# A row sum bound by its loads: one whole first load in front of the entry barrier, a wait for the ends moved forward, and a store of its own for the first seven blocks

## The chip, the cores and the metric

The kernel runs on one core of one Trainium2 chip. The time is device microseconds of that core. A profile adds its own clock: "span" is the time from the first to the last instruction on the core, about 1.8 us less than the device time. All runs quoted here are of the fast state, with a granted clock of 1.0.

Some words. A DMA moves data between memory and the core; SyncE issues it, and the core's 16 DMA engines carry it in packets. A semaphore is a counter on which an engine waits; the semaphore of a DMA tells that its data has landed. The entry barrier is the place at the program's start where all engines wait for each other. A nop is an instruction that does nothing, but can wait.

## The reference

```python
batch, seq, dim = 32, 512, 1024          # x: float32, standard normal
def reference(x, multiplier):            # multiplier = 0.5
    return (np.sum(x, axis=-1) * multiplier).astype(np.float32)
```

So 16,384 rows of 4 KB (67.1 MB) are read, and 64 KB of sums are written.

## The kernel before

Each of the 128 partitions owns 128 consecutive rows. A block is 16 rows of every partition, 8.4 MB; there are eight blocks and three buffers. In blocks 0 to 6 VectorE (DVE) sums the first eight rows with one reduction and ScalarE (ACT) the other eight with one ACTIVATE each. The last block comes in five pieces that get smaller and smaller. All DMAs are issued by SyncE (SP).

```python
    x_rows = x_flat.rearrange("(p c) d -> p c d", p=P)
    out_view = out.rearrange("b s -> (b s)").rearrange("(p c) -> p c", p=P)
    ...
    for b in range(n_blocks - 1):
        c0 = b * B
        t = x_pool.tile([P, B, D], fp32, name="xb")
        step = 4 if b == 0 else 1
        for q in range(step):                       # block 0: every fourth partition
            nc.sync.dma_start(
                out=t[q:P:step], in_=x_rows[q:P:step, c0 : c0 + B, :]
            )
        h = B // 2
        nc.vector.reduce_sum(out=sums[:, c0 : c0 + h], in_=t[:, 0:h, :], ...)
        nc.vector.tensor_single_scalar(out=res[:, c0 : c0 + h], ...)
        for r in range(h, B):
            act_row(t, r, c0 + r)
    ...
    pieces = [(0, 8), (8, 13), (13, 15)]            # the last block, rows;
    ...                                             # row 15 in columns 0:640, 640:1024
    nc.sync.dma_start(out=out_view, in_=res)        # 64 KB, after everything

    def start_loads_at_entry(nc_):
        ...          # moves SP's leading loads that wait for nothing in front of
        ...          # SP's part of the entry barrier
            for i in own:
                if not is_load(i) or i.sync_info.on_wait:
                    break
                lead.append(i)
```

Six loads can go without waiting: four pieces of block 0, block 1, block 2. All six are issued in front of the entry barrier.

## Time and profile before

| | before |
|---|---|
| device time | 163.19 us median of three (163.19 to 163.27) |
| span of the profiled run | 161.6 us (that run took 163.42 us) |
| DVE, ACT busy | 42% each |
| loads' share of the chain of waits | 85% |
| mean DMA rate | 416 GB/s |

The page says at once what the bound is. These are its lines for the busy share in 40 slices (tenths) and the DMA rate, of the kernel before:

```profile
DVE  0000039800596007940099101990039800597453
ACT  0000039900595007920099101990039700596852
...
DMA  6989989988989988998998997997997997999990
GB/s 260 519 373 406 519 373 405 519 389 389 519 357 422 519 389 389 519 405 373 519 422 359 519 438 341 519 438 341 519 438 341 519 438 341 430 438 398 424 375 28
```

DVE and ACT stand still more than half of the time (busy 42% each); the DMA engines, whose packets fill 96.7% of 16 engines' span, hardly ever do, except in the first slice and in the last. The trace's packet records give the pace: a 64 KB packet, one partition's share of a block, takes 2.418 us in the median on each of 16 engines. That is 27.1 GB/s per engine and, by multiplication, 434 GB/s together. With the engines that busy (a share of 0.98 from 10 to 40 us) nothing in the middle can be gained by waiting less. What is open is the head, before all 16 engines move data, and the tail, after the last data.

The tail, from the end of the chain that ended last (start, length, what) in the kernel before:

```profile
110.47 47.68 DMA xb<-in_x_dram
158.15 0.02 issue
158.18 0.49 DVE xb L57
...
158.76 0.42 DVE xb L57
159.18 0.01 DVEq L167
```

DVE is done at 159.18 us; the store and the closing barrier take the other 2.44 us to the span's end at 161.62. The store's own lines from the view of its source line, with durations in ns and starts in us:

```profile
L108 SPq EVENT_SEMAPHORE  x1: 17/17/17, 159.2 to 159.2; - x1
L108 SPq DMA_DIRECT2D out_dram<-res x1: 348/348/348, 159.3 to 159.3; - x1
```

The head: the DMA view cut to the first 4 us, in 40 slices of 0.1 us, and the first issue on SP's queue (start, length):

```profile
GB/s 0 0 0 0 0 0 0 0 0 0 0 0 0 1311 0 1966 1311 0 0 655 1311 1311 0 1311 0 655 655 0 0 0 0 0 0 0 0 0 0 0 0 0
...
0.00 0.54 SPq L73 DMA_DIRECT2D xb<-in_x_dram  x1
```

Each packet is counted in the slice in which it starts, so this row shows the starts: 655 is one packet of 64 KB. The first of the 16 engines starts at 1.36 us (slice 14), the last at 2.68 us. And the first reduction, which waits for all of block 0 (its last piece landed at 22.75 us, and DVE then went through waits for all four), starts at 22.87 us:

```profile
22.87 8.69 DVE L77 TENSOR_REDUCE sums<-xb 128x8 f32<-128x8192 f32 x1 [22.87 <-DMA xb<-in_x_dram]
```

### The profile page before, as it was taken

Reading aid. Unit: us, or ns where it says so; the run is one execution under the profiler, and the core shown is the slowest. Engines: PE = TensorE matmul, PEld = TensorE weight load, DVE = VectorE, ACT = ScalarE, POOL = GpSimd, SP = SyncE. Lnnn points to the kernel's source line nnn. Section 1 sums busy time; section 2 is a strip of 40 time slices with the busy share of each in tenths; the row PEclk is TensorE's granted clock in tenths of the full one; section 3 lists DMA queues with packets and bytes.
Section 4 is the critical chain, followed back from the end, with each engine's and each line's share of the span. In section 5 each row is a group of like instructions: output and inputs, shape, how many; then the busy total and the mean of one; then the engine's idle time right before and its main releaser. Section 6 shows DMA issues by size and latency. Waiting matters only on the chain.

```text
span 161.6 us, 242 instructions
## 1 busy us (share of the span) xinstructions
DVE 68.1 (42%) x34; ACT 67.9 (42%) x127; POOL 0.2 (0%) x4
## 2 busy tenths in 40 slices
DVE  0000039800596007940099101990039800597453
ACT  0000039900595007920099101990039700596852
POOL 0000000000000000000000000000000000000000
DMA  6989989988989988998998997997997997999990
GB/s 260 519 373 406 519 373 405 519 389 389 519 357 422 519 389 389 519 405 373 519 422 359 519 438 341 519 438 341 519 438 341 519 438 341 430 438 398 424 375 28
DMA packets 1921, 67.18 MB, mean 416 GB/s; under 512 B 256, under 2 KB 512, under 8 KB 640
## 3 DMA queue, kind: packets, MB, share of 16 engines
q1 hardware_dynamic: 1920, 67.18, 96.7%
q14 instruction: 1, 0.01, 0.0%
HBM read 67.11 MB, written 0.07 MB: 416 GB/s over the span
## 4 chain that ended last, share of the span: by engine, by line
DMA 85%; DVE 11%; SPq 2%; issue 0%; DVEq 0%
DMA xb<-in_x_dram 85%; DVE sums L77 11%; SPq L73 2%; SPq L94 1%; DVE xb L57 1%; DVE part L57 0%; DVEq L167 0%
## 5 line engine op out<-in xcount | busy, mean ns | idle before, releaser
L77 DVE TENSOR_REDUCE sums<-xb 128x8 f32<-128x8192 f32 x7 | 60.8, 8686 | 85.7 <-DMA xb<-in_x_dram 85.7
L47 ACT ACTIVATE xb<-xb 128x1024 f32<-128x1024 f32 x63 | 65.6, 1043 | 67.8 <-DMA xb<-in_x_dram 67.8
L47 ACT ACTIVATION_READ_ACCUMULATOR xb<-xb 128x1 f32 x63 | 11.8, 187 | 0.0
L47 ACT ACT_TABLE_LOAD x1 | 1.3, 1283 | 22.8 <-DMA xb<-in_x_dram 22.8
L57 DVE CUSTOM_DVE_ANT_0 xb<-xb 128x512 f32<-128x512 f32 (+1 forms) x9 | 5.6, 667 | 5.1 <-DMA xb<-in_x_dram 4.9
L80 DVE TENSOR_SCALAR res<-sums 128x8 f32<-128x8 f32 x7 | 1.2, 172 | 0.2
L57 DVE DVE_READ_ACCUMULATOR2_ANT res<- 128x1 f32 x9 | 0.7, 83 | 0.0
L57 DVE CUSTOM_DVE_ANT_0 xb<-xb,part 128x192 f32<-128x192 f32 x1 | 0.4, 418 | 0.1
L153 POOL MEMSET const-bfloat16-1.0<- 128x1 bf16 x1 | 0.1, 102 | 0.0
L153 POOL MEMSET const-uint8-127<- 128x1 uint8 x1 | 0.1, 102 | 0.0
L153 POOL MEMSET const-float32-0.0<- 128x1 f32 x1 | 0.1, 99 | 0.2 <-issue 0.2
L153 POOL MEMSET const-float32-1.0<- 128x1 f32 x1 | 0.1, 99 | 0.0
L57 DVE DVE_READ_ACCUMULATOR2_ANT part<- 128x1 f32 x1 | 0.1, 81 | 0.0
## 6 DMA issues: line engine op xcount, KB each, us to landing
xb<-in_x_dram SPq DMA_DIRECT2D x1, 4096.0 KB, 39.6
xb<-in_x_dram SPq DMA_DIRECT2D x1, 2560.0 KB, 45.4
xb<-in_x_dram SPq DMA_DIRECT2D x1, 1024.0 KB, 47.4
xb<-in_x_dram SPq DMA_DIRECT2D x1, 320.0 KB, 47.7
xb<-in_x_dram SPq DMA_DIRECT2D x1, 192.0 KB, 47.6
xb<-in_x_dram SPq DMA_DIRECT2D x10, 43.8
out_dram<-res SPq DMA_DIRECT2D x1, 64.0 KB, 1.5
```

Of the source, the lines that this page charges most:

```text
L47: nc.scalar.activation(out=t[:, r, :], in_=t[:, r, :], func=mybir.ActivationFunctionType.Copy, scale=mul, accum_out=res[:, col : col + 1],)
L57: nc.vector.tensor_tensor_reduce(out=t[:, r, lo:mid], in0=t[:, r, lo:mid], in1=t[:, r, mid:hi], scale=mul, scalar=start, op0=ADD, op1=ADD, ...
L73: nc.sync.dma_start(out=t[q:P:step], in_=x_rows[q:P:step, c0 : c0 + B, :])
L77: nc.vector.reduce_sum(out=sums[:, c0 : c0 + h], in_=t[:, 0:h, :], axis=mybir.AxisListType.X)
L80: nc.vector.tensor_single_scalar(out=res[:, c0 : c0 + h], in_=sums[:, c0 : c0 + h], scalar=mul, op=mybir.AluOpType.mult,)
L94: nc.sync.dma_start(out=t[:, lo:hi, :], in_=x_rows[:, c0 + lo : c0 + hi, :])
L153: nc = _bacc.Bacc("TRN2", target_bir_lowering=False, num_devices=1)
```

## The change

Its intent has three parts. Block 0 comes as one load, which alone stands in front of the entry barrier. The results of blocks 0 to 6 are stored by a DMA of their own while the last block is still coming, so that only 8 KB are left to store at the end. And a nop on SP waits for the loads and for ACT's last row before the last store, so that these waits are not left to the end of the program.

```diff
-        step = 4 if b == 0 else 1
-        for q in range(step):
-            nc.sync.dma_start(
-                out=t[q:P:step], in_=x_rows[q:P:step, c0 : c0 + B, :]
-            )
+        loads.append(nc.sync.dma_start(out=t, in_=x_rows[:, c0 : c0 + B, :]))
 ...
+    c1 = c0
+    nc.sync.dma_start(out=out_view[:, 0:c1], in_=res[:, 0:c1])
     on_act = {4, 5, 6, 7, 11, 12, 14}
 ...
-    nc.sync.dma_start(out=out_view, in_=res)
+    seen = nc.sync.nop()
+    for i in loads[-8:] + acts[-1:]:
+        tc.add_manual_dep(seen.ins, i.ins.name, ..., reason="ends seen early")
+    store = nc.sync.dma_start(out=out_view[:, c1:], in_=res[:, c1:])
+    tc.add_manual_dep(store.ins, seen.ins.name, ..., reason="in this order")
 ...
             for i in own:
-                if not is_load(i) or i.sync_info.on_wait:
+                if not is_load(i) or i.sync_info.on_wait or len(lead) == 1:
                     break
```

More of the change, by code (lines that the diff above doesn't have):

```diff
@@ L44 @@
     part = res_pool.tile([P, 1], fp32, name="part")
+    loads = []
+    acts = []
     def act_row(t, r, col):
-        nc.scalar.activation(
+        acts.append(nc.scalar.activation(
             out=t[:, r, :],
@@ L52, in act_row @@
             accum_out=res[:, col : col + 1],
-        )
+        ))
     def dve_span(t, r, lo, hi, dst, start=0.0):
@@ L70 @@
         t = x_pool.tile([P, B, D], fp32, name="xb")
-        step = 4 if b == 0 else 1
-        for q in range(step):
-            nc.sync.dma_start(
-                out=t[q:P:step], in_=x_rows[q:P:step, c0 : c0 + B, :]
-            )
+        loads.append(nc.sync.dma_start(out=t, in_=x_rows[:, c0 : c0 + B, :]))
         h = B // 2
@@ L93 @@
     for lo, hi in pieces:
-        nc.sync.dma_start(out=t[:, lo:hi, :], in_=x_rows[:, c0 + lo : c0 + hi, :])
+        loads.append(
+            nc.sync.dma_start(
+                out=t[:, lo:hi, :], in_=x_rows[:, c0 + lo : c0 + hi, :]
+            )
+        )
     for lo, hi in ((0, cut), (cut, D)):
-        nc.sync.dma_start(
-            out=t[:, B - 1, lo:hi], in_=x_rows[:, c0 + B - 1, lo:hi]
-        )
+        loads.append(
+            nc.sync.dma_start(
+                out=t[:, B - 1, lo:hi], in_=x_rows[:, c0 + B - 1, lo:hi]
+            )
+        )
+    c1 = c0
+    nc.sync.dma_start(out=out_view[:, 0:c1], in_=res[:, 0:c1])
     on_act = {4, 5, 6, 7, 11, 12, 14}
@@ L106, with start_load_at_entry @@
     dve_span(t, B - 1, cut, D, res[:, rows - 1 : rows], start=part)
-    nc.sync.dma_start(out=out_view, in_=res)
-    def start_loads_at_entry(nc_):
+    seen = nc.sync.nop()
+    for i in loads[-8:] + acts[-1:]:
+        tc.add_manual_dep(
+            seen.ins,
+            i.ins.name,
+            mybir.DependencyInfo(mybir.DependencyClass.Sync, mybir.DependencyReason.DATA),
+            reason="ends seen early",
+        )
+    store = nc.sync.dma_start(out=out_view[:, c1:], in_=res[:, c1:])
+    tc.add_manual_dep(
+        store.ins,
+        seen.ins.name,
+        mybir.DependencyInfo(mybir.DependencyClass.NoSync, mybir.DependencyReason.SCHED_ONLY),
+        reason="in this order",
+    )
+    def start_load_at_entry(nc_):
         entry, *rest = nc_.main_func.blocks
@@ L134, in start_loads_at_entry @@
             return
-    nc.at_finalize(start_loads_at_entry)
+    nc.at_finalize(start_load_at_entry)
 _INS = ['x', 'multiplier']
```

## The prediction

> **What bounds the kernel.** The load stream. The page's first two parts: DVE and ACT are busy 42% each, the DMA slices read 9 (96.7% of 16 engines' span), 67.18 MB at 416 GB/s. The chain of waits is 85% loads; DVE enters it only as the release of a buffer whose next load already queues behind others. The trace's packet records: a 64 KB packet takes 2.418 us (median), 27.1 GB/s on each of 16 engines. [...] An engine's 64 packets' worth need 154.8 us, so only about 6.9 us of the span are open: start and end.
>
> **Start.** The first packets of the 16 engines begin between 1.355 and 2.683 us; [...]last packets of the last load end between 157.05 and 158.18 us, the same 1.1 us spread. [...] Six load issues take 3.74 us there (0.54 to 0.76 each), and the starts fall while issues 3 to 5 are written. [...]the final store's packets begin 0.85 us after its issue, on all engines within about 0.2 us. I think a single first load, with nothing issued behind it until the barrier (about 1 us later by the barrier instructions' times), starts the engines closer together, perhaps by 1.2 to 2.2 us: estimated gain 0.4 us, anything from -0.5[...] to +1.0.
>
> **ACT's table load** (1.28 us at 22.84 us) waits in "before" for three of the four first loads; after, only the first ACTIVATE waits, so it hides at the start. Block 3's load may be issued 1 us earlier, but 40 us of loads queue before it: worth 0. Loads two and three, after the barrier, have 20 us of slack.
>
> **End.** Last landing 158.15, DVE's two pieces to 159.18 (unchanged), store issue 0.35, landing 1.5 us from issue (160.8), closing barrier 0.75. SP's waits for the other loads (six of 28 ns after the store's issue) already run inside the store's flight, so seeing them early gains at most about 0.05 us. The last store falls from 64 to 8 KB; its 27 ns packets x 8 per engine are 0.22 us of the flight, shrinking to perhaps 0.08: gain 0.1. The rest is fixed (this trace: 0.85 us before the first packet, about 0.35 us after the last). The early store is issued near 148 us behind the last loads in the same rings; its 8 packets per engine (estimate 0.2 us) come after the loads and before the last store: worth 0.
>
> **Sum.** 163.19 - 0.4 - 0.15 = 162.6 us, 8 in 10 within 161.8 to 163.5. Faster by over 2%: 0.03; within 2%: 0.94; slower by over 2%: 0.03.
>
> **What would show it.** Right: first packets of all engines within under 1 us; last landing at about 157.6 instead of 158.15; ACT_TABLE_LOAD before 3 us; the last store landing about 1.4 us from issue; DVE, ACT groups unchanged. Wrong: first packets still spread over 1.3 us (then only the end's 0.1 to 0.2 us comes), or the last landing later than 158.2.
>
> **What would make it wrong.** The cold start may be a cost of each engine's first read rather than of competing issues (no gain)[...]. The stores' 448- and 64-byte rows might write slowly.

Passages are cut where it is marked. What the runs show of the middle is that no kernel below has a median packet under 2.418 us. 163.19 - 0.4 - 0.15 = 162.64, put down as 162.6. The 0.4 us is the author's estimate: a last first packet at about 2.2 instead of 2.683 us would be 0.48 us earlier, and it was assumed, not shown, that the end moves with it. The 0.15 is the estimated 0.05 for the waits and 0.1 for the small store.

Three of its numbers are loose: the sixth issue took 0.46 us and not 0.54 or more, the first packets spread over 1.33 us and not 1.1, and the waits between the store's issue and the drain are five (one of 17 and four of 28 ns), of which four ran before the landing. "The same rings" are the one queue, q1, that the DMA view shows for all loads and stores.

## The result

| | before | after |
|---|---|---|
| device time, six fast runs each | 163.25 us (163.19 to 163.28) | 162.96 us (162.91 to 163.22) |
| ratio, 95% interval | | 0.9985 (0.9972 to 0.9998) |
| span of the profiled run | 161.6 us | 161.1 us |

All outputs are right. A ratio here is the mean time of one kernel's fast runs over the mean of the other's in the same rounds, so it is not quite the ratio of the medians quoted. In a later job the changed kernel ran again (e12): 162.90 us against 163.28, ratio 0.9979 (0.9967 to 0.9991). So the change gains about 0.3 us, 0.2%. The time lies in the predicted range; the predicted gain (0.55 us) was about twice the measured one. Note that the profiled run of before took 163.42 us, slower than its timed runs, and that of after 162.91, its fastest: the half microsecond between the two spans flatters the change.

The same views of the changed kernel. The end of its chain, its last store, its first 4 us and its first issue, its first reduction, and ACT's first instructions:

```profile
110.01 47.72 DMA xb<-in_x_dram
157.73 0.02 issue
157.75 0.49 DVE xb L60
...
158.32 0.42 DVE xb L60
158.74 0.01 DVEq L190
```

```profile
L125 SPq EVENT_SEMAPHORE  x2: 28/28/28, 158.8 to 158.8; - x2
L125 SPq DMA_DIRECT2D out_dram<-res x1: 344/344/344, 158.9 to 158.9; - x1
```

```profile
GB/s 0 0 0 0 0 0 0 0 0 0 2621 1966 655 655 0 655 1311 1311 1311 0 0 0 0 0 0 0 0 0 0 0 0 0 0 0 0 0 0 0 0 0
...
0.00 0.38 SPq L74 DMA_DIRECT2D xb<-in_x_dram  x1
...
22.55 8.69 DVE L76 TENSOR_REDUCE sums<-xb 128x8 f32<-128x8192 f32 x1 [22.55 <-DMA xb<-in_x_dram]
```

```profile
0.79 1.28 ACT L50 ACT_TABLE_LOAD   x1 [0.79 <-PEq L176]
22.55 1.06 ACT L50 ACTIVATE xb<-xb 128x1024 f32<-128x1024 f32 x1 [20.48 <-DMA xb<-in_x_dram]
```

The first packet starts at 1.02 us instead of 1.36, the first reduction at 22.55 us instead of 22.87 (block 0 landed at 22.53 instead of 22.75), the last load lands at 157.73 instead of 158.15, and DVE ends at 158.74 instead of 159.18. The tail from there to the span's end is 161.12 - 158.74 = 2.38 us instead of 2.44. ACT's table load (1.28 us) has moved from 22.84 to 0.79 us and is hidden. So the gain is in the load stream; 0.22 us of it is there when block 0 has landed, the rest comes later in these two profiles. The tail, at which two of the three parts of the change aim, gives 0.06 us. The experiments ask why the head starts earlier and why the tail gives so little.

### The profile page after: what moved, and what is told of

It is laid out like the page before. It is cut to its first block, busy times and chain, and to the rows that moved or that the text cites. A ratio compares the mean times of both kernels' runs of the same rounds, so it can differ in the third digit from the quotient of the medians.

```text
span 161.1 us, 236 instructions
## 1 busy us (share of the span) xinstructions
DVE 68.1 (42%) x34; ACT 67.9 (42%) x127; POOL 0.2 (0%) x4
## 4 chain that ended last, share of the span: by engine, by line
DMA 86%; DVE 11%; SPq 1%; issue 0%; DVEq 0%
DMA xb<-in_x_dram 86%; DVE sums L76 11%; SPq L94 1%; DVE xb L60 1%; SPq L74 0%; DVE part L60 0%; DVEq L190 0%
## 6 DMA issues: line engine op xcount, KB each, us to landing
out_dram<-res SPq DMA_DIRECT2D x1, 56.0 KB, 10.8
```

## The experiments

All diffs below are against the changed kernel. For the head there were two theories. P is that of the prediction: issues that follow each other compete, so the engines start late and far apart, and it helps to put one load alone in front of the barrier. T came from the two traces: in before the mean second packet of the engines took 2.53 us, in after the mean fifth 2.59 us, the others from the second on 2.42 or 2.43. T says that an engine's first read of a far region is slow and that cutting block 0 in four brings two such reads early. For the tail, A says that the head has most of the gain, its rival that the tail has it.

### The start alone (e1)

```diff
-    c1 = c0
-    nc.sync.dma_start(out=out_view[:, 0:c1], in_=res[:, 0:c1])
 ...                                      # the nop and its dependencies too
-    store = nc.sync.dma_start(out=out_view[:, c1:], in_=res[:, c1:])
+    nc.sync.dma_start(out=out_view, in_=res)
```

> The new start (one whole first load in front of the barrier) with the old end (one 64 KB store). Theory A, most of the gain is at the start: 0.15 to 0.25 us quicker than before, last landing about 157.75 us as in the changed kernel, tail from DVE's end to the span's end 2.44 us as before. Rival, the gain is the end's (smaller last store): within 0.05 us of before.

Measured: 163.30 us (163.09 to 163.64) against 163.33, ratio 0.9997 (0.9985 to 1.0010). By the time alone the rival would have won. But the profile shows the early landing: block 0 there at 22.30 us, last landing 157.63, DVE's end 158.68. This was the quickest of its five runs (163.09), so it shows the head at its best. The loss is behind that: from DVE's end to the span's end 2.63 us instead of before's 2.44, although the store is the same 64 KB and is issued equally soon (0.07 us) after DVE's end. These are SP's instructions between the store's landing and the closing drain; first before, then e1:

```profile
L167 SPq EVENT_SEMAPHORE  x1: 28/28/28, 160.8 to 160.8; - x1
L167 SPq DRAIN  x1: 7/7/7, 160.9 to 160.9; - x1
```

```profile
L174 SPq EVENT_SEMAPHORE  x4: 28/28/28, 160.3 to 160.5; - x4
L174 SPq DRAIN  x1: 7/7/7, 160.6 to 160.6; - x1
```

The last wait in before, and all four in e1, end after the landing; in e1 they are about 62 ns apart. The built programs of before and e1 say why. In them each DMA gets one of eight completion semaphores in turn, and the program's end waits for all of them in one order, the same in both, mostly two per instruction:

```
S3 | S4,S2 | S5,S1 | S6,S0 | S7,DVE | drain: ACT
```

In before 15 loads precede the store, so it has semaphore 7 and its wait is in the last pair. The whole first load leaves 12 loads; the store gets semaphore 4, its wait is in the second pair, and three more instructions run after the landing. Nothing in the source says so. The trace shows the inserted EVENT_SEMAPHORE instructions, at 28 ns each and about 62 ns from one to the next.

### The end alone (e2)

```diff
-        loads.append(nc.sync.dma_start(out=t, in_=x_rows[:, c0 : c0 + B, :]))
+        step = 4 if b == 0 else 1
+        for q in range(step):
+            loads.append(nc.sync.dma_start(
+                out=t[q:P:step], in_=x_rows[q:P:step, c0 : c0 + B, :]))
 ...
-                if not is_load(i) or i.sync_info.on_wait or len(lead) == 1:
+                if not is_load(i) or i.sync_info.on_wait:
```

> The old start (load cut in four, three blocks in front of the barrier) with the new end (early store, ends seen early). Theory A: 0.05 to 0.10 us quicker than before; with the start's gain it adds up to the changed kernel's 0.25. Rival: it has all of the gain.

Measured: 163.21 us (163.13 to 163.38) against 163.24, ratio 0.9996 (0.9984 to 1.0009): no resolved gain. The tail of its profile is 2.36 us, 0.08 less than before's, as theory A expected; a gain of that size can't be told from the noise. Theory A's other half, that the two parts add up to the whole, is not met by the times: each alone gives about nothing, both together 0.3 us. The waits of e1 explain 0.19 us of that; the intervals leave room for the rest.

### All three whole loads in front of the barrier (e3)

```diff
-                if not is_load(i) or i.sync_info.on_wait or len(lead) == 1:
+                if not is_load(i) or i.sync_info.on_wait:
```

> As the changed kernel, but all three first loads, each whole, in front of the barrier. If the place of the barrier matters (competing issues, or the barrier itself), the start falls back towards before: 0.2 us slower than the changed kernel. If only the way the first load is cut matters, the same as the changed kernel within 0.05 us. First packets at 1.0 to 1.9 us in both cases by my guess.

Measured: 162.94 us (162.85 to 163.16) against 163.33, ratio 0.9975 (0.9963 to 0.9988): as quick as the changed kernel. The second and third issue follow at 0.44 and 0.90 us, just before the engines' starts, and the starts don't mind (the first at 1.0 us, the last at 2.3):

```profile
GB/s 0 0 0 0 0 0 0 0 0 0 2621 1966 655 1311 0 655 1311 0 655 0 0 655 0 655 0 0 0 0 0 0 0 0 0 0 0 0 0 0 0 0
```

So "alone in front of the barrier" is worth nothing here, and theory P falls: two issues that follow the first whole load did not delay it (162.94 us here, 162.90 to 162.96 for the changed kernel).

### The cut in four behind the new barrier (e4)

```diff
+        step = 4 if b == 0 else 1        # as in e2
 ...
-                if not is_load(i) or i.sync_info.on_wait or len(lead) == 1:
+                if not is_load(i) or i.sync_info.on_wait or len(lead) == 4:
```

> As the changed kernel, but the first load is cut in four interleaved pieces as before, all four in front of the barrier, loads two and three behind it. Theory of competing issues (P): little gain, since four issues still follow each other: first packets spread 1.2 us or more. Theory of first touches (T: a DMA engine's first read of a far region is slow, and the cut in four makes packets one and two both first reads): the second packet's mean stays near 2.53 us and the time is about 0.2 us longer than the changed kernel's.

Measured: 163.38 us (163.04 to 163.73) against 163.33, ratio 1.0001 (0.9987 to 1.0014). With the cut, all of the gain is gone. The first packets start late, at 1.52 us, and the first reduction starts at 22.82 us:

```profile
GB/s 0 0 0 0 0 0 0 0 0 0 0 0 0 0 0 655 1966 0 655 1311 0 1311 1311 655 0 0 1311 655 0 655 0 0 0 0 0 0 0 0 0 0
```

The second packet's mean was 2.46 us, not 2.53, and in e2, with the same cut, 2.42. In the same way the fifth packet of the whole load was 2.42 us in e3, e6, e7 and e12. T's slow packets were thus a matter of single profiles, and T falls too. In after they are one burst: eight packets that started between 11.46 and 12.19 us took 2.69 to 2.94 us. Bursts of seven or eight packets that start within 0.7 to 0.8 us stand in other profiles at other moments: at 40.6 us in before (2.62 to 2.96 us), 25.8 in e12, 35.6 in e6, 31.1 in e4, none in e7 and e8. Their cause is open. What e3 and e4 leave is that the cut itself matters. I call that theory S: the shape of the first load (32 partitions, every fourth) makes it start late.

### The cut in eight (e5)

```diff
+        step = 8 if b == 0 else 1        # else as in e2
 ...
-                if not is_load(i) or i.sync_info.on_wait or len(lead) == 1:
+                if not is_load(i) or i.sync_info.on_wait:
```

> As the changed kernel, but the first load is cut in eight, one partition per engine and piece,[...] and all loads that need not wait stand in front of the barrier. Theory P (competing issues): at least as slow as before at the start, first packets spread over 1.3 us, last landing 158.1 or later. Theory T (order of first reads): the slow packets are the first and the fifth of each engine as in the changed kernel, packet two near 2.43 us, and the last landing is within 0.15 us of the changed kernel's 157.73.

Measured: 184.58 us against 163.33, 13% slower, which neither theory had expected; the test said nothing about P and T. The rate from 10 to 40 us, first before, then e5 (the row gives the window, its length, the busy engines, the clock, the DMA share and the rate):

```profile
10.00:40.00 30.00, 8.86 (x2) 9.70 (x17) 0.00 (x0) 1.00 0.98 424
```

```profile
10.00:40.00 30.00, 0.00 (x0) 0.00 (x0) 0.00 (x0) 1.00 1.02 210
```

All 16 DMA engines are as busy as before (a share of 1.02 against 0.98), and half as much arrives (210 against 424 GB/s): a 64 KB packet takes 5.11 us instead of 2.42, 2.1 times as long. The rate is back at its old level once whole loads follow: the page's slices from 46 to 82 us read 401 to 458 GB/s. The cause is not shown. A piece has 16 partitions, every eighth, and the rows that it reads lie 4 MB apart in the input, instead of 512 KB in a whole load; no run separates the two. The cut in four, every fourth partition with rows 2 MB apart, has packets that settle at 2.42 us. So a cut by partitions has to be measured. The first packet starts late here too, at 1.37 us.

### The nop taken away (e6), and the early store taken away (e7)

e6 removes the nop and keeps the two stores; e7 keeps the nop and has one store of 64 KB at the end.

```diff
 # e6
-    seen = nc.sync.nop()
-    ...                                  # and both dependencies
-    store = nc.sync.dma_start(out=out_view[:, c1:], in_=res[:, c1:])
+    nc.sync.dma_start(out=out_view[:, c1:], in_=res[:, c1:])
 # e7
-    c1 = c0
-    nc.sync.dma_start(out=out_view[:, 0:c1], in_=res[:, 0:c1])
-    store = nc.sync.dma_start(out=out_view[:, c1:], in_=res[:, c1:])
+    store = nc.sync.dma_start(out=out_view, in_=res)
```

> The changed kernel without the nop that waits for the loads and ACT, early store kept. Theory: the nop brings at most 0.05 us, since those waits would run while the last store is in flight; it may cost 0.08 us, since in the changed kernel the store is issued 0.16 us after DVE's end, before 0.08. Expected: the same as the changed kernel within 0.08 us, store issued 0.08 us after DVE's end. Rival (the intent of the change): 0.1 us or more slower.

> The changed kernel with the nop, but one 64 KB store at the end. Theory: loses the 0.1 us of the smaller store's flight (issue to landing 1.5 instead of 1.4 us) and nothing else: 0.1 us slower than the changed kernel.

Measured: e6 163.00 us (162.95 to 163.17), ratio 0.9985; e7 162.86 us (162.84 to 163.02), ratio 0.9975; before 163.24 in the same job. Neither is slower than the changed kernel's 162.90 to 162.96 by a resolved amount, and e7, without the early store, is not slower at all. The traces give the parts that the times don't resolve (ns, from the packet and instruction records of one profile each):

| | store issued after DVE's end | last packet of the store after its issue | from there to the span's end | tail |
|---|---|---|---|---|
| before (one store, semaphore 7) | 74 | 1193 | 1169 | 2436 |
| e1 (one store, semaphore 4) | 74 | 1194 | 1361 | 2629 |
| e7 (one store, nop) | 92 | 1194 | 1162 | 2448 |
| e6 (two stores, no nop) | 64 | 1040 | 1313 | 2417 |
| after (two stores, nop) | 155 | 1038 | 1187 | 2380 |

The small store does what it should: its flight is 0.155 us shorter. The nop removes the waits behind the landing, about 0.2 us of e1's end and 0.13 of e6's. But together they put one more wait instruction between DVE's end and the last store, which in the built program waits for DVE and one load in one instruction, for another load and its own semaphore's turn before in the next, and for ACT. The lines of the last store shown above have it: two waits of 28 ns where before has one of 17, and 155 ns instead of 74 until the issue. That is half of what the small store gains. Shortening this order of waits was not tried.

### Another place for the same store, without the nop (e10)

If the place of the wait is the cause, then e1 must get its old tail back once its store has semaphore 7 again. e10 is e1 with block 2 loaded in four pieces of rows, so that 15 loads precede the store.

```diff
-        loads.append(nc.sync.dma_start(out=t, in_=x_rows[:, c0 : c0 + B, :]))
+        step = 4 if b == 2 else 1
+        g = B // step
+        for q in range(step):
+            loads.append(nc.sync.dma_start(
+                out=t[:, q * g : (q + 1) * g, :],
+                in_=x_rows[:, c0 + q * g : c0 + (q + 1) * g, :]))
```

> As e1 (new start, one 64 KB store, no nop), but block 2 is loaded in four pieces of rows, so that 15 loads precede the store as in the kernel before and the store gets the same completion semaphore (the eighth) as there. Theory W: the start saves about 0.4 us, and e1 lost it at the end, because its store had the fifth semaphore and three waits of about 62 ns each stood behind the wait for it. Then the tail from DVE's end to the span's end is 2.44 us as in the kernel before, instead of e1's 2.63, and the time is 162.95 to 163.1. Rival: the start brings nothing and e1's early landing was luck of one profile; then 163.25 or more.

Measured: tail 2436 ns, before's to the nanosecond, with one wait behind the landing:

```profile
L182 SPq EVENT_SEMAPHORE  x1: 28/28/28, 160.7 to 160.7; - x1
L182 SPq DRAIN  x1: 7/7/7, 160.7 to 160.7; - x1
```

The mechanism of the tail is shown. The time is 163.19 us (162.99 to 163.24) against 163.28, ratio 0.9990 (0.9977 to 1.0003), outside the expected 162.95 to 163.1. The trace says where the rest went: block 0 was there at 22.13 us, but the last engine needed 19.95 us for block 2 instead of 19.33 (it ended block 1 at 41.08 and block 2 at 61.03 us). Its first three pieces took 4.862 us each, where two packets of 64 KB take 4.836, and the fourth 5.36. In the fourth, eight packets that started between 56.15 and 56.89 us took 0.72 to 1.21 us, where the others took 0.61. That is a burst like those of e4's section, and those hit kernels without such a cut too. So the 0.6 us are lost in this profile, but that the cut by rows causes them is not shown.

### Four pieces over all partitions (e11)

```diff
+        step = 4 if b == 0 else 1        # pieces of rows, as in e10
 ...
-                if not is_load(i) or i.sync_info.on_wait or len(lead) == 1:
+                if not is_load(i) or i.sync_info.on_wait or len(lead) == 4:
```

> As e4 (four loads in front of the barrier, the rest behind it), but the four pieces of block 0 are cut by rows, each over all 128 partitions with 16 KB runs, instead of by every fourth partition. If it is the number of issues that makes the cut start late, the first packets begin at 1.3 us or later as in e4 (1.52) and before (1.36), and the time is about 163.35 as e4's. If it is the shape of the first load (32 of 128 partitions, stride 4), the first issue takes about 0.38 us instead of 0.55, the first packets begin at about 1.0 us, and the time is within 0.1 us of the changed kernel's.

Measured: 163.28 us (163.08 to 164.12) against 163.28, ratio 1.0007 (0.9990 to 1.0023). The first half of the expectation holds for theory S, the first issue took 0.37 us and the first packet started at 1.02 us, though four issues stand in a row as in e4:

```profile
GB/s 0 0 0 0 0 0 0 0 0 0 655 655 164 164 164 164 164 0 0 0 0 328 655 655 328 655 0 328 655 655 328 655 0 328 492 492 492 655 164 328
```

The packets are of 16 KB here, so 164 is one of them. The time did not follow. By the last completions of the four pieces, the last engine was 0.76, 0.74 and 0.71 us ahead of before's (7.14 against 7.90, 12.00 against 12.74, 16.87 against 17.57), and then ended the fourth piece at 22.81 against 22.41: 5.94 us for the fourth piece, where the second and the third took 4.86 and 4.87. Again it is a burst, the largest of all: eight packets that started between 16.16 and 16.87 us, at the beginning of the fourth piece, took 1.2 to 2.0 us instead of 0.61. Both kernels cut by rows have it in their fourth piece, so the cut may have a part in it; with one profile of each, that stays open. So S is supported for the start of the packets, and by the times only in that the kernels with the cut by partitions (before, e2, e4) have medians of 163.2 to 163.4 us and those with a whole first load (after, e3, e6, e7, e12) of 162.9 to 163.0; e1, with its waits, and e10, with its burst, lie outside this. That any cut in four loses the gain, whatever its shape, is not excluded by the times.

### Blocks that lie together in memory (e8, and again e13 beside e12)

A block of the kernel before is 128 pieces of 64 KB that lie 512 KB apart. e8 gives each block 8.4 MB in one stretch, by another split of rows over partitions and blocks; the result is the same.

```diff
-    x_rows = x_flat.rearrange("(p c) d -> p c d", p=P)
-    out_view = out.rearrange("b s -> (b s)").rearrange("(p c) -> p c", p=P)
+    x_blocks = x_flat.rearrange("(n p r) d -> n p r d", p=P, r=B)
+    out_view = out.rearrange("b s -> (b s)").rearrange("(n p r) -> p n r", p=P, r=B)
 ...
-        loads.append(nc.sync.dma_start(out=t, in_=x_rows[:, c0 : c0 + B, :]))
+        loads.append(nc.sync.dma_start(out=t, in_=x_blocks[b]))
 ...                                      # the last block's pieces and the stores too
```

> The changed kernel with another split of the rows: each block is one contiguous 8 MB of the input, instead of 128 pieces of 64 KB that lie 512 KB apart. Theory T (slow first reads of a far region, per engine): the fifth packet is not slow any more (2.42 instead of 2.59 us mean), but each block brings new regions: packets 9, 17, 25 and so on get slow, and if every engine pays 0.1 to 0.2 us each time the time grows by 0.7 to 1.4 us. If the cost is shared by the engines, the time changes by under 0.3 us. Rival (a fixed start-up cost of each engine, nothing to do with addresses): only the first packet is slow, the fifth may stay slow, no other.

Measured: 162.70 us (162.58 to 162.81) against 163.24, ratio 0.9962 (0.9950 to 0.9975). But for one at 86.6 us (see below) no packet after an engine's first is slow against the median of 2.418 us, at no block's start, so no cost of new regions is visible in this profile; this too speaks against T. But the first packets end closer together, the last at 4.66 us instead of 5.26, and block 0 is there earlier, as the first reduction shows:

```profile
21.95 8.69 DVE L76 TENSOR_REDUCE sums<-xb 128x8 f32<-128x8192 f32 x1 [21.95 <-DMA xb<-in_x_dram]
```

To compare it with the changed kernel on one chip, both ran again.

> The changed kernel unaltered, for a comparison on the same chip with the contiguous one: 162.9 to 163.05 us.

> e8 unaltered (each block one contiguous 8 MB). If its gain is real, 0.2 to 0.3 us quicker than the changed kernel in this job, with all engines' first packets done by about 4.7 us instead of 5.1 to 5.3. If it was luck: equal to the changed kernel within 0.1 us.

Measured: e12 162.90 us (162.67 to 163.37), ratio 0.9979; e13 162.87 us (162.63 to 162.97), ratio 0.9971. The early block is there again (21.86 us in e13, 22.16 in e12; last first packet 4.57 and 4.86 us), the time difference is not: 0.03 us of medians, 0.13 of means, inside the spread. Part of it was lost later: by the last completion of a block, e13 was 0.48 us ahead of e12 at block 2 (60.15 against 60.63 us) and only 0.03 us ahead at block 4 (99.27 against 99.30). The packet records show how. In every profile but e5's, one DMA engine carries one 8 KB packet of the kind "instruction" (0.31 us) between 84 and 88 us, and the load packet that starts at its end takes 2.66 to 2.80 us (e5 has the same at 108 us). In e13 that packet came at 84.09 us and the next one ended at 87.18; five more of 2.418 us make 99.27, which is when the last engine of block 4 ended. In after, the same count gives 99.42, before the last engine (99.51), and nothing was lost. The records don't name the engine, so this rests on the count. The contiguous kernel is the quickest that I ran, by 0.4 to 0.5 us of the medians against before, but whether it beats the changed kernel is not settled.

## Why the prediction was right or wrong

**The bound: right.** Packets of 64 KB take 2.418 us in the median of all kernels but for e5's block 0; what is gained is gained in the load stream's head (0.36 us by the means at block 0) and at the tail (0.06 us). That the middle could not get quicker by any change was not shown.

**"a single first load, with nothing issued behind it until the barrier [...] starts the engines closer together": size right, mechanism wrong.** The estimate was 0.4 us. DVE ends, in the mean of one profile each, at 159.17 us in the kernels whose first load is cut by partitions (before, e2, e4: 159.19, 158.99, 159.33) and at 158.69 us in those with a whole one and no other cut (after, e1, e3, e6, e7, e12): 0.48 us. At the landing of block 0 the same means are 22.69 and 22.34 us, so 0.36 us is the head's. But it is no matter of competing issues, as e3 shows, and the starts are only a little closer together: the spread is 0.84 us in after's profile, which looked like a success, but 1.08 to 1.31 in e1, e3, e6, e7 and e12, against 1.33 to 1.46 with the cut. What moves is the whole group: the first start from 1.33 to 1.52 down to 0.98 to 1.02 us, the last from 2.68 to 2.98 down to 1.86 to 2.32, together with a first issue of 0.38 instead of 0.54 us. From the end of that issue to the first packet it is 0.62 to 0.65 us with the whole load and 0.79 to 0.97 with the cut. This goes with the shape of the first load (e4 against e11: the first packet at 1.52 and at 1.02 us), while the time of e11 shows no gain. What in the shape delays it, 32 partitions, the stride of four or the larger distance in the input, was not separated.

**The table load, and loads two and three after the barrier: right.** The table load starts at 0.79 us; that it is worth nothing, because the loads bind, is argued; no run moves it alone.

**"seeing them early gains at most about 0.05 us": right in size, and for a wrong reason.** In the changed kernel the nop is worth 2417 - 2380 = 37 ns of tail. The prediction reasoned that the waits "already run inside the store's flight". That is true of before, by luck of the semaphore's turn; the new start takes three loads away and would have put three waits behind the landing. Without the nop and with one store this costs 0.19 us (e1, e10). The parts of the change depend on each other, and I had costed them one by one.

**The small store: right in its own term, wrong in the sum.** Predicted gain 0.1 us, measured 0.155 of flight (its packets of 64 bytes take 11 ns in the median, those of 512 bytes in before 27, and the early store's of 448 bytes 25, so no short row took longer than a long one); but the store is issued 81 ns later, behind one more wait. The tail as a whole gives 0.06 us where 0.15 was predicted.

**The early store "worth 0" for the loads: right.** It was issued at 147.60 us and landed 10.8 us later, behind the last loads, before the last store was issued at 158.90. The last load landed at 157.48 to 157.76 us in the profiles with it and a whole first load (after, e3, e6, e12), at 157.59 and 157.63 in those without (e7, e1).

**The sum.** 162.6 us was predicted, 162.96 and 162.90 measured. The terms of the traces, 0.48 and 0.06, would give 0.54; the timed gain is 0.24 and 0.34 by the means. The profiles are one execution each, and not of middling ones: the three with the cut were on average 0.06 us slower than the medians of their kernels, the six with a whole load 0.08 us quicker. Without this, 0.54 would be 0.40. The rest is not assigned to a cause; the bursts and the instruction packet disturb the stream by some tenths at moments that differ from profile to profile. In e1 the head (0.36 us by the means at block 0) less its tail (0.19) should have left about 0.17 us; 0.03 was measured, with an interval that reaches to 0.25.

## What to carry to other kernels

When a kernel is bound by its loads, look at when the first packets start and what stands behind the last landing. Here both depended on things the source doesn't show: the first packet started at 0.98 to 1.02 or at 1.33 to 1.52 us with the shape of the first DMA, and the tail was 2.44 or 2.63 us with the turn of the store's completion semaphore. Three loads fewer changed which semaphore the last store got, so read SP's waits after the last landing again after every change in the number of DMAs. A cut that is meant to be neutral has to be measured: every eighth partition halved the rate (210 against 424 GB/s), and a cut by rows brought no gain in time in two trials (163.19 and 163.28 us against 163.28). Where single profiles are compared, look for bursts of slow packets and for the instruction packet first: in the bursts here seven or eight packets of 64 KB took 2.57 to 2.96 instead of 2.42 us (before, after, e4, e6, e12), those of 16 KB up to 1.2 (e10) and 2.0 us (e11) instead of 0.61, and the packet after the instruction packet took 2.66 to 2.80 us.
